# Summing the adaLN products over partitions: VectorE block transposes in place of column-tiled products

## Chip, cores and metric

One core of a Trainium2 chip runs the kernel; the other cores have nothing to do. The metric is the device time of one execution, in microseconds (us). Work is spread over TensorE (PE in the profile; PEld are its weight loads), VectorE (DVE), ScalarE (ACT), GpSimd (POOL), and SyncE (SP), which issues the loads.

## What is computed

Two layers of a conditioned decoder trunk on a sequence of 256 tokens, width 1024, in float32. Each layer has three sublayers: a half-step SwiGLU FFN, a token mixer, another half-step SwiGLU FFN. In front of each stands an RMS norm with a shift and a scale, behind it a gate, and these come from a vector `c`:

```python
mod = (silu(c) @ ada_w[l] + ada_b[l]).reshape(B, 3, 3, 1, D)     # 3 sublayers x (shift, scale, gate)
n = modulate(rmsnorm(h, norm_g[l, 0]), mod[:, 0, 0], mod[:, 0, 1])
h = h + 0.5 * mod[:, 0, 2] * swiglu(n, ffn_w_in[l, 0], ffn_w_out[l, 0])
```

So there are 2 x 3 x 3 = 18 vectors of 1024 values, each a product of a vector of 1024 with a 1024 x 1024 matrix: 4 MB of weights for each and little arithmetic. Two of the 18, shift and scale of the first sublayer, are wanted at once and have a path of their own; the other 16 are the "sets" that this case is about.

## The kernel before

All activations are kept transposed: channels on the 128 partitions in 8 blocks, tokens along the free dimension. Weights come in tiles of 128x1024 float32 through one stream (`Stream`), in one fixed order, 512 KB each. For a product in nearly full precision each tile is split into a high part (`hi`, ScalarE, line 151) and the rest (`lo`, VectorE, line 152), and each block product is three TensorE passes: hi with hi, lo with hi, hi with lo. The stream loads ahead up to RAW_MAX_X = 9 tiles and splits ahead up to SPLIT_AHEAD_X = 7 tiles while the slots of the mixer's tiles are lent to it (`lend`), less otherwise.

The adaLN weights run through the same stream, between the others (`ada_plan` says under which sublayer which set is loaded: five sets under the first FFN, one under the first mixer, four under the second FFN, five under the third, one under the last). An adaLN tile is not split: VectorE multiplies it with `silu(c)` per partition and adds it up in `acc[si, m]`, 128x1024 (lines 274 and 277, 8 tiles to a set). What is left is the sum of `acc` over the 128 partitions. `ada_step` does it two steps of its clock after the last tile of a set, called between blocks of products; `ada_flush` brings the results of a sublayer into the layout that is wanted, channels on partitions, and adds bias and the rest (`md`).

In `ada_step` four products of 128x32 weights, one for each quarter of the columns of `acc`, go to the four column tiles of the array. The weights `hot` are zero but for one column of ones, so set k lands in row k of each tile's 32 output rows; ScalarE or VectorE collects this into `rows`. In `ada_flush` two TensorE transposes turn `rows`, and VectorE picks each set's 8 columns.

The order on TensorE, SyncE and GpSimd is that of the program (`manual_schedule`). VectorE and ScalarE are ordered by a planner at build time, by priority (program order less what `tc.high_priority` gives) among what it takes to be ready; at run time each engine goes through its queue in order. ScalarE is in program order in `start()` too.

In `ffn`, `in_mm(j)` are the 48 products of one block of the input projection (line 660), `evac(j)` the SwiGLU of it (lines 626 to 628 and 597, 598), `out_mm(j)` the 24 products of a block of the output projection (line 606). `ada_step` stands behind `out_mm`, `ada_flush` ahead of the last `out_mm`, which takes two blocks together. `mix` ends in the same way, with step and flush inside its last products. `enter` then needs `md`: it updates h with the gate (line 477), forms `uhi` and `ulo` (lines 479 and 472), and starts the next sublayer's products (line 494). `finish` does the same at the end (line 564).

In `start()`, VectorE forms the first two sets by the own path (lines 398, 400, 776 to 784). There `const_load` loads the constants `cst_t[:, 128:]` (line 407), which hold, among others, four 32x32 identities on top of each other (C_SEL).

Of the kernel before, what the change touches and what calls it, by code (L numbers as in the profile page):

```python
# [18 lines left out]
F32 = mybir.dt.float32  # L19
F32R = mybir.dt.float32r  # L20
AF = mybir.ActivationFunctionType
ALU = mybir.AluOpType
AX = mybir.AxisListType.X
# [12 lines left out]
PRIO_C, PRIO_R, PRIO_T, PRIO_A, PRIO_H, PRIO_M = 300, 200, 400, 50, 50, 300  # L36
# [17 lines left out]
C_VE, C_VM, C_SEL, C_CAUS, C_TRIL, C_BM, C_END = 930, 1058, 1186, 1346, 1474, 1602, 1606  # L54
# [129 lines left out]
def trunk(ctx, tc, xT, pk, cst, ada0, win7, ada, win, wou, mixw, mixv, w1, mp, wsT, lngb, bs, out):  # L184
    nc = tc.nc
    V, A, T, G = nc.vector, nc.scalar, nc.tensor, nc.gpsimd

    cp = ctx.enter_context(tc.tile_pool(name="cp", bufs=1))
# [4 lines left out]
    tp = ctx.enter_context(tc.tile_pool(name="tp", bufs=1))  # L193
# [6 lines left out]
    def uid():  # L200
        cnt["id"] += 1
        return cnt["id"]

    def bank(tag):
        return ps.tile([128, 512], F32, tag=tag, name=f"{tag}_{uid()}")

    def rbank():
        cnt["R"] += 1
        return bank(f"R{cnt['R'] % 4}")

    def s1(dt=F32, tag="s1", bufs=8, n=256):
        return tp.tile([128, n], dt, tag=tag, bufs=bufs, name=f"{tag}_{uid()}")
# [11 lines left out]
    def s2():  # L224
        return s1(F32, "s2", 4, 512)

    def small(n, tag, dt=F32, bufs=2):
        return tp.tile([128, n], dt, tag=tag, bufs=bufs, name=f"{tag}_{uid()}")
# [7 lines left out]
    cst_t = cp.tile([128, C_END], F32, name="cst_t")  # L236
# [4 lines left out]
    ident = cst_t[:, C_ID:C_ID + 128]  # L241
# [3 lines left out]
    nc.sync.dma_start(pk_t, pk)  # L245
    V.memset(ones, 1.0)
    V.memset(mhalf, -0.5)
    hot = cp.tile([128, 64], F32, name="hot")
    V.memset(hot, 0.0)
    V.memset(hot[:, 31:32], 1.0)  # L250
    sel = cp.tile([128, 2], F32, name="sel")
    V.memset(sel, 0.0)
    for t in range(4):
# [3 lines left out]
    def norm_g(si):  # L257
        return pk_t[:, 8 + si * 8:16 + si * 8]
# [3 lines left out]
    def ada_b(si):  # L262
        return pk_t[:, 64 + si * 24:88 + si * 24]


    acc = {}
    mods = {}
    ready, summed, rows, clock = [], [], {}, [0]
# [13 lines left out]
    def ada_step(now=False):  # L282

        clock[0] += 1
        while ready and (now or clock[0] >= ready[0][2]):
            si, m, _ = ready.pop(0)
            k = len(summed)
            p = rbank()
            for t in range(4):
                T.matmul(p[32 * t:32 * t + 32, 0:256], hot[:, 31 - k:63 - k], acc[si, m][:, t * 256:(t + 1) * 256],  # L290
                         start=True, stop=True, tile_position=(0, 32 * t))
            with tc.high_priority(PRIO_M):
                if k == 0:
                    rows["t"] = tp.tile([128, 256], F32, tag="adas", name=f"adas{si}_{m}")
                    A.activation(rows["t"], p[:, 0:256], AF.Copy)
                else:
                    V.tensor_add(rows["t"], rows["t"], p[:, 0:256])
            summed.append((si, m))

    def ada_flush():  # L300

        p = rbank()
        for f in range(2):
            T.transpose(p[:, f * 128:(f + 1) * 128], rows["t"][:, f * 128:(f + 1) * 128], ident)
        with tc.high_priority(PRIO_M):
            for k, (si, m) in enumerate(summed):
                t = cp.tile([128, 8], F32, tag=f"md{si}_{m}", name=f"md{si}_{m}")
                v = p[:, 0:256].rearrange("p (f t r) -> p t f r", f=2, r=32)[:, :, :, k]
                V.tensor_add(t.rearrange("p (t f) -> p t f", f=2), v,
                             ada_b(si)[:, m * 8:(m + 1) * 8].rearrange("p (t f) -> p t f", f=2))  # L310
                if m == 1:
                    V.scalar_tensor_tensor(t, t, 1.0, norm_g(si), op0=ALU.add, op1=ALU.mult)
                elif m == 2:
                    V.tensor_scalar(t, t, 0.5, None, op0=ALU.mult)
                mods[si, m] = t
        summed.clear()
# [88 lines left out]

    def const_load():
        nc.sync.dma_start(cst_t[:, 128:], cst[:, 128:])

    for kb in range(8):
        for k in ((0,), (1, 2), (3,), (4,), (5,), (6,), (7,), ())[kb]:  # L410
            items += [ada0_item(k, 0), ada0_item(k, 1)]
            ada0_last.append(len(items) - 1)
        items += [("w", win7[kb, :, 0:1024], 1024), ("w", win7[kb, :, 1024:], 768)]
        if kb == 3:
            items.append(("call", const_load, ()))
# [199 lines left out]
    def ffn(si, prev):  # L615
# [21 lines left out]
        if si == 0:  # L637
            with tc.manual_schedule(engines=START_ENGINES):
                x, zb = start()
            for j in range(4):  # L640
                evac(j, zb[j])
            accs = [bank(f"A{i}") for i in range(4)]
            for j in range(NS - 1):
                out_mm(j)
                if j + 4 < NS:
                    evac(j + 4, zb[j + 4])
                st.more()
                ada_step()
# [56 lines left out]
        for j in range(NS if si == 0 else 4, NF):  # L705
            r = in_mm(j)
            evac(j, r)
            st.more()
            for k in outs_after(si, j):
                out_mm(k)  # L710
                if k < NF - TAIL:
                    st.more()
                ada_step(k >= NF - TAIL)
        if summed:
            ada_flush()
# [111 lines left out]
    def mix(si, l, prev):  # L827
# [441 lines left out]
        for kb in range(8 - WGROUP):  # L1269
            acc_mm(accs, [(st.next(), mhi[:, kb], mlo[:, kb])], kb == 0, False)  # L1270
            st.more()
            if kb >= 2:
                ada_step()
        Ws = [(st.next(), mhi[:, kb], mlo[:, kb]) for kb in range(8 - WGROUP, 8)]
        acc_mm(accs, Ws, False, True, lambda db: ada_step(True) if db == 0 else ada_flush() if db == 3 and summed else None)
        return accs

# [126 lines left out]
```

## Time and profile before

| | us |
|---|---|
| three runs without profile | 1122.38, 1124.91, 1126.12 (median 1124.91) |
| profiled execution | 1121.94 |
| its span, first to last instruction | 1119.8 |
| TensorE, VectorE, ScalarE busy in the span | 1109.5, 875.0, 601.1 |

A span is one execution as the profiler saw it. TensorE's matmuls are pipelined and overlap in the record, so a duration of one (some 277 ns for 256 columns) is longer than the distance from one to the next. The chain of work is followed back from the last instruction, at each step to what released it or to the instruction before it on its engine; it tells which work the end hangs on.

### The profile page before, as it was taken

How to read it: one execution, taken by the hardware profiler on the slowest of the kernel's cores; microseconds unless marked ns; L12 is line 12 of the kernel's file. 1: busy time of each engine (PE TensorE's matmuls, PEld its weight loads, DVE VectorE, ACT ScalarE, POOL GpSimd, SP SyncE). 2: the span in 40 equal slices, each digit the busy share in tenths (PEclk: the TensorE clock that was granted, in tenths of full speed). 3: DMA queues.
4: the chain of work that ended last, by engine and by line, in shares of the span. 5: the costliest groups of instructions: out<-in, count | busy, mean ns of one | idle time of the engine just before them, and what ended most of it. 6: DMA issues, size and time to landing. Idle time of an engine off the chain costs nothing.

```text
span 1119.8 us, 23472 instructions
## 1 busy us (share of the span) xinstructions
PE 1109.5 (99%) x9542; PEld 1068.0 (95%) x9542; DVE 875.0 (78%) x1495; ACT 601.1 (54%) x1014; POOL 11.2 (1%) x15
## 2 busy tenths in 40 slices
PE   9999999999999999999999999999999999999997
PEld 8999999989999999999999999998899999999997
DVE  6898888998868799787599987868876689755643
ACT  4463435675665655444464443558566657544543
POOL 0000000000000000000000000000000000000000
PEclk9999999999999999999999999999999999999999
DMA  9999889756453669888547977965633373866601
GB/s 370 403 336 353 301 316 362 274 191 228 170 180 123 247 234 407 322 323 314 193 148 293 408 290 286 341 244 188 217 133 132 133 276 139 310 216 243 218 31 38
DMA packets 80379, 278.06 MB, mean 248 GB/s; under 512 B 10768, under 2 KB 11280, under 8 KB 80272
## 3 DMA queue, kind: packets, MB, share of 16 engines
q1 hardware_dynamic: 80272, 276.58, 67.6%
q8 instruction: 74, 1.21, 0.4%
q14 instruction: 33, 0.27, 0.1%
HBM read 275.49 MB, written 1.05 MB: 247 GB/s over the span
## 4 chain that ended last, share of the span: by engine, by line
PE 61%; DVE 1%; DMA 1%; ACT 1%; issue 0%; POOL 0%; DVEq 0%; SPq 0%; ACTq 0%; POOLq 0%
PE R L660 28%; PE A L606 16%; PE A L856 4%; PE R L494 2%; PE A L843 2%; PE A L660 1%; DMA raw<-in_win 1%; PE A L1071 1%; PE R L843 1%; PE R L1071 1%; DVE lo L152 1%; PE R L1208 1%; PE R L1176 1%; PE R L290 1%; PE R L856 1%; PE A L1218 0%
## 5 line engine op out<-in xcount | busy, mean ns | idle before, releaser
L152 DVE TENSOR_TENSOR lo<-raw,hi 128x1024 fp32r<-128x1024 f32 x366 | 443.0, 1215 | 115.9 <-ACT hi L151 72.7
L151 ACT ACTIVATE hi<-raw 128x1024 fp32r<-128x1024 f32 x368 | 381.7, 1048 | 242.3 <-PE R L660 57.6
L606 PE MATMUL A<-s1r,hi 128*128 128x256 f32 x1408 | 252.7, 277 | 0.0
L660 PE MATMUL R<-nhi,hi 128*128 128x256 f32 x1152 | 226.1, 278 | 0.0
L660 PE MATMUL R<-nhi,lo 128*128 128x256 f32 x1152 | 224.9, 276 | 0.0
L660 PE MATMUL R<-nlo,hi 128*128 128x256 f32 x1152 | 224.5, 276 | 0.0
L606 PEld LDWEIGHTS A<-s1r,hi 128*128 128x128 f32 x1408 | 218.0, 188 | 0.6 <-ACT hi L151 0.4
L606 PE MATMUL A<-s1r,lo 128*128 128x256 f32 x704 | 194.9, 277 | 0.0
L660 PEld LDWEIGHTS R<-nhi,hi 128*128 128x128 f32 x1152 | 173.5, 188 | 5.8 <-issue 5.8
L660 PEld LDWEIGHTS R<-nhi,lo 128*128 128x128 f32 x1152 | 173.9, 188 | 0.0
L660 PEld LDWEIGHTS R<-nlo,hi 128*128 128x128 f32 x1152 | 173.6, 188 | 0.0
L277 DVE SCALAR_TENSOR_TENSOR acc<-raw,sc,acc 128x1024 f32<-128x1024 f32 x112 | 143.3, 1279 | 8.6 <-DMA raw<-in_ada 8.2
L606 PEld LDWEIGHTS A<-s1r,lo 128*128 128x128 f32 x704 | 132.2, 188 | 0.0
L626 ACT ACTIVATE s<-R 128x256 f32<-128x256 f32 x75 | 28.3, 378 | 132.8 <-PE R L660 132.8
L856 PE MATMUL A<-nhi,hi 128*128 128x256 f32 x256 | 72.7, 284 | 0.0
L856 PE MATMUL A<-nlo,hi 128*128 128x256 f32 x256 | 70.8, 277 | 0.0
L856 PE MATMUL A<-nhi,lo 128*128 128x256 f32 x256 | 70.8, 277 | 0.0
L628 DVE TENSOR_TENSOR s<-s,R 128x256 f32<-128x256 f32 x75 | 31.2, 416 | 39.1 <-ACT s L626 39.1
L597 ACT ACTIVATE s1r<-s 128x256 fp32r<-128x256 f32 x88 | 36.0, 412 | 35.6 <-DVE s L628 33.9
L856 PEld LDWEIGHTS A<-nhi,hi 128*128 128x128 f32 x256 | 48.1, 188 | 2.1 <-issue 0.3
L856 PEld LDWEIGHTS A<-nhi,lo 128*128 128x128 f32 x256 | 48.2, 188 | 0.0
L856 PEld LDWEIGHTS A<-nlo,hi 128*128 128x128 f32 x256 | 48.1, 188 | 0.0
(274 smaller groups left out, 1598.0 us busy)
## 6 DMA issues: line engine op xcount, KB each, us to landing
raw<-in_win SPq DMA_DIRECT2D x170, 512.0 KB, 5.9
raw<-in_ada SPq DMA_DIRECT2D x144, 512.0 KB, 6.1
raw<-in_mixw SPq DMA_DIRECT2D x92, 512.0 KB, 3.6
raw<-in_wou SPq DMA_DIRECT2D x88, 512.0 KB, 5.9
w<-in_w SPq DMA_DIRECT2D x8, 512.0 KB, 7.4
raw<-in_mixv SPq DMA_DIRECT2D x8, 512.0 KB, 4.9
raw<-in_win SPq DMA_DIRECT2D x8, 384.0 KB, 9.6
h<-in_xT SPq DMA_DIRECT2D x2, 512.0 KB, 4.3
```

Source lines behind the costliest of these rows:

```text
L151: self.nc.scalar.activation(hv, rv, AF.Copy)
L152: self.nc.vector.tensor_sub(lv, rv, hv.bitcast(F32))
L277: V.scalar_tensor_tensor(a, raw[:, :D], sc[:, kb:kb + 1], a, op0=ALU.mult, op1=ALU.add)
L494: T.matmul(ub[u][b][:, 0:SU], w(u, (0, 1, 0)[part], kb, b), (uhi, uhi, ulo)[part][:, kb], start=(kb == 0 and part == 0), stop=(kb == 7 and ...
L597: A.activation(hi_out, src, AF.Copy)
L606: T.matmul(accs[db // 2][:, (db % 2) * S:(db % 2 + 1) * S], w[:, db * 128:(db + 1) * 128], xx, start=(first and i == 0 and p == 0 and db % ...
L626: A.activation(s_, r[:, 0:S], AF.Silu)
L628: V.tensor_mul(g_, s_, r[:, S:2 * S])
L660: T.matmul(r[:, ab * S:(ab + 1) * S], W[:, c0:c0 + 128], xx[:, k], start=(i == 0 and ab == 0), stop=(i == 23), skip_group_check=True)
L843: T.matmul(banks[tt][i][:, 0:cn], xx[:, kb, tt * 128:(tt + 1) * 128], w[:, k, c0:c0 + cn], start=(kb == 0 and p == 0), stop=(kb == 7 and p ...
L856: T.matmul(r[:, b * S:(b + 1) * S], w[:, k], xx[:, k], start=(b == 0 and k == 0 and p == 0), stop=(k == 7 and p == 2), skip_group_check=True)
L1071: T.matmul(r[:, 0:S], w[:, k, b * 128:(b + 1) * 128], xx[:, k], start=(n == 0), stop=(n == 11))
```

## The change

`ada_step` no longer uses TensorE. For each half of `acc`, VectorE transposes it in blocks of 32x32 within 128x512 and adds up each block's rows (32 columns each), which leaves in `rows`, 128 x (set, 32), the sums over each group of 32 partitions. `ada_flush` adds the four groups with one fp32 product for all sets of the sublayer: weights `sel4`, 128x128, which are four identities of 32 beside and on top of each other, and 32 columns for each set. The result has all channels on every group of 32 partitions; four VectorE copies, one a group, pick what belongs there, and the additions of the bias follow. `hot` goes; `sel4` is filled by four VectorE copies out of `cst_t` in `const_load`. The order of the calls and of the loads stays. The first two sets keep their own column-tiled products in `start()`.

```diff
-    hot = cp.tile([128, 64], F32, name="hot")
-    V.memset(hot, 0.0)
-    V.memset(hot[:, 31:32], 1.0)
+    sel4 = cp.tile([128, 128], F32, name="sel4")
...
-            p = rbank()
-            for t in range(4):
-                T.matmul(p[32 * t:32 * t + 32, 0:256], hot[:, 31 - k:63 - k], acc[si, m][:, t * 256:(t + 1) * 256],
-                         start=True, stop=True, tile_position=(0, 32 * t))
-            with tc.high_priority(PRIO_M):
-                if k == 0:
-                    rows["t"] = tp.tile([128, 256], F32, tag="adas", name=f"adas{si}_{m}")
-                    A.activation(rows["t"], p[:, 0:256], AF.Copy)
-                else:
-                    V.tensor_add(rows["t"], rows["t"], p[:, 0:256])
+            a = acc[si, m]
+            if k == 0:
+                rows["t"] = tp.tile([128, 5, 32], F32, tag="adas", name=f"adas{si}_{m}")
+            for c in range(2):
+                t = s2()
+                V.transpose(t, a[:, c * 512:(c + 1) * 512])
+                V.tensor_reduce(rows["t"][:, k, c * 16:(c + 1) * 16], t.rearrange("p (j r) -> p j r", r=32), axis=AX, op=ALU.add)
...
-        for f in range(2):
-            T.transpose(p[:, f * 128:(f + 1) * 128], rows["t"][:, f * 128:(f + 1) * 128], ident)
+        n = len(summed)
+        T.matmul(p[:, 0:n * 32], sel4, rows["t"][:, 0:n].rearrange("p k j -> p (k j)"), start=True, stop=True)
         with tc.high_priority(PRIO_M):
+            v = p[:, 0:n * 32].rearrange("p (k f q) -> p q k f", k=n, q=4)
+            u = small(40, "adac", bufs=1)
+            uv = u[:, 0:n * 8].rearrange("p (k f) -> p k f", f=8)
+            for q in range(4):
+                V.tensor_copy(uv[32 * q:32 * q + 32], v[32 * q:32 * q + 32, q])
...
-                V.tensor_add(t.rearrange("p (t f) -> p t f", f=2), v,
-                             ada_b(si)[:, m * 8:(m + 1) * 8].rearrange("p (t f) -> p t f", f=2))
+                V.tensor_add(t, uv[:, k], ada_b(si)[:, m * 8:(m + 1) * 8])
...
     def const_load():
         nc.sync.dma_start(cst_t[:, 128:], cst[:, 128:])
+        for q in range(4):
+            V.tensor_copy(sel4[:, 32 * q:32 * q + 32], cst_t[:, C_SEL:C_SEL + 32])
```

## Rows read from the trace of the kernel before

**Rows 1.** The page, part 1: busy us, share of the span, instructions.

```profile
PE 1109.5 (99%) x9542; PEld 1068.0 (95%) x9542; DVE 875.0 (78%) x1495; ACT 601.1 (54%) x1014; POOL 11.2 (1%) x15
```

**Rows 2.** The chain of work in order of time: start us, us, what.

```profile
392.47 1.13 DVE lo L152
...
424.22 5.44 PE R L660 x48
...
448.70 0.57 PE R L290 x8
449.27 5.65 PE R L660 x48
...
818.40 1.70 PE R L1104 x16
```

**Rows 3.** Stretches: us, busy us (instructions) of each engine, TensorE clock, DMA share, GB/s.

```profile
20.00:34.00 14.00, 14.00 (x126) 12.50 (x127) 13.93 (x31) 6.46 (x10) 0.00 (x0) 1.00 1.03 407
...
84.00:196.00 112.00, 112.00 (x983) 109.83 (x982) 94.13 (x103) 47.79 (x67) 0.00 (x0) 1.00 0.91 333
616.00:728.00 112.00, 112.00 (x996) 109.31 (x995) 94.41 (x104) 49.98 (x68) 0.00 (x0) 1.00 0.88 331
728.00:749.00 21.00, 21.00 (x188) 21.00 (x187) 10.83 (x16) 9.60 (x14) 0.00 (x0) 1.00 0.66 233
```

**Rows 4.** Timeline of TensorE, three places: start us, us, engine, line, operation, shapes.

```profile
28.82 0.40 PE L792 MATMUL A<-nhi,lo 128*128 128x256 f32 x2
...
203.91 0.27 PE L304 MATMUL R<-cst_t,adas 128*128 128x128 f32 x1
...
449.20 0.50 PE L660 MATMUL R<-nhi,hi 128*128 128x256 f32 x2
449.54 0.39 PE L660 MATMUL R<-nhi,lo 128*128 128x256 f32 x2
```

**Rows 5.** Groups by line and shape: busy us, mean ns, idle before and releaser.

```profile
L290 PE MATMUL R<-acc,hot 128*32 128x256 f32 x128 | 10.2, 391 | 0.0
...
L297 DVE TENSOR_TENSOR adas<-adas,R 128x256 f32<-128x256 f32 x11 | 4.6, 415 | 1.8 <-PE R L290 1.8
...
L995 DVE BATCH_NORM_STATS2 bst<-vz 128x6 f32<-128x512 f32 x4 | 2.6, 686 | 2.2 <-ACT vz L984 2.2
...
L1021 DVE TENSOR_SCALAR vz<-vz,mv,vr 128x512 f32<-128x512 f32 x4 | 2.1, 534 | 0.4 <-POOL vr L1001 0.4
...
L1129 DVE TENSOR_REDUCE sm<-s 128x16 f32<-128x256 f32 x2 | 0.8, 408 | 0.0
...
L1015 DVE COPY kcs<-R 32x64 f32<-32x64 f32 x2 | 0.4, 202 | 0.0
```

**Rows 6.** VectorE's waits, 84 to 196 us, then the whole span: total us, times, longest.

```profile
DVE s L628 <- ACT s L626: 12.8, 12, 2.2
...
DVE s L731 <- DMA h<-in_xT: 3.2, 1, 3.2
```

**Rows 7.** The chain of work in the last 22 us: start us, us, what.

```profile
1103.72 0.22 PE R L304 x2
...
1105.38 0.49 DVE h L564
```

**Rows 8.** Timeline of VectorE, four places; in brackets the idle time before and its releaser.

```profile
25.07 1.22 DVE L152 TENSOR_TENSOR lo<-raw,hi 128x1024 fp32r<-128x1024 f32 x1
...
201.20 0.42 DVE L297 TENSOR_TENSOR adas<-adas,R 128x256 f32<-128x256 f32 x1 [0.39 <-PE R L290]
...
378.43 0.17 DVE L309 TENSOR_TENSOR md<-R,pk_t 128x8 f32<-128x8 f32 x1 [3.70 <-PE R L304]
...
1104.18 0.17 DVE L314 TENSOR_SCALAR md<-md 128x8 f32<-128x8 f32 x1
```

**Rows 9.** The line that loads the constants: SyncE's issue, and issue to landing.

```profile
L407 SPq DMA_DIRECT2D cst_t<-in_cst x1: 328/328/328, 21.3 to 21.3; - x1
...
DMA to landing us min/median/max: 10.1/10.1/10.1
```

More of the change, by code (lines that the diff above doesn't have):

```diff
@@ L302, in ada_flush @@
         p = rbank()
-        for f in range(2):
-            T.transpose(p[:, f * 128:(f + 1) * 128], rows["t"][:, f * 128:(f + 1) * 128], ident)
+        n = len(summed)
+        T.matmul(p[:, 0:n * 32], sel4, rows["t"][:, 0:n].rearrange("p k j -> p (k j)"), start=True, stop=True)
         with tc.high_priority(PRIO_M):
+            v = p[:, 0:n * 32].rearrange("p (k f q) -> p q k f", k=n, q=4)
[3 more added lines that the diff above has]
+                V.tensor_copy(uv[32 * q:32 * q + 32], v[32 * q:32 * q + 32, q])
             for k, (si, m) in enumerate(summed):
                 t = cp.tile([128, 8], F32, tag=f"md{si}_{m}", name=f"md{si}_{m}")
-                v = p[:, 0:256].rearrange("p (f t r) -> p t f r", f=2, r=32)[:, :, :, k]
-                V.tensor_add(t.rearrange("p (t f) -> p t f", f=2), v,
-                             ada_b(si)[:, m * 8:(m + 1) * 8].rearrange("p (t f) -> p t f", f=2))
+                V.tensor_add(t, uv[:, k], ada_b(si)[:, m * 8:(m + 1) * 8])
                 if m == 1:
```

## The prediction

> **What bounds the kernel now.** I read the page first: TensorE is busy for 99% of a span of 1119.8 us, VectorE for 78%, ScalarE for 54% [rows 1]. A busy TensorE may still be one that waits with a matmul open, so I went on to the chain of work in order of time. In the FFN stages it is TensorE from one matmul to the next: 5.44 us for each 48 products of a projection, with nothing between [rows 2]. So a microsecond taken out of TensorE's own queue there is a microsecond of the time, as long as what feeds TensorE keeps up. VectorE feeds it (each weight tile needs a subtraction on line 152), and so does the DMA; that is the question I then put to the table by stretches, where TensorE's granted clock is 1.00 [rows 3].
>
> **What leaves TensorE.** In the same chain each step of the adaLN sums (line 290) stands as 0.57 us, and the 48 products behind it take 5.65 instead of 5.44 us [rows 2]. The timeline shows where: the first two products behind the group take 0.50 us, the next two 0.39 us as usual [rows 4]. A set costs 0.57 + 0.21 = 0.78 us. Line 290 has 128 records [rows 5], 8 in a set [rows 2], so there are 16 sets: 16 x 0.78 = 12.5 us. I count all of it as gained, since TensorE has no gap around these groups.
>
> [...] By the rows, the eight records hold TensorE for 0.57 us and the products behind them for 0.21 us more [rows 2]. [...]
>
> **What comes onto VectorE.** A set gets two block transposes of 128x512 and two sums of 128x512 into 128x16. No row shows a transpose. For the sums there are rows of half the size, 0.408 us for 128x256; statistics over 128x512 took 0.686 us, a scaling of 128x512 0.534 us [rows 5]. From below a transpose costs what the scaling does, 0.53 us; from above I allow it four passes, 4 x 0.68 = 2.7 us. I take 0.68 us, the rows of the same shape that go through it once. The set then costs 4 x 0.68 = 2.7 us; the addition of line 297, 0.414 us in 11 of the 16 sets [rows 5], goes, and five ScalarE copies. Net 2.3 to 2.7 us a set, some 39 us in all, on an engine with 245 us of idle time.
>
> [...]
>
> Does it fit where the sets lie? From 84 to 196 us VectorE was busy for 94.1 of 112 us [rows 3]. Four of the first sublayer's five sets are in there: 4 x 2.4 = 9.6 us, and TensorE's gain makes the stretch 3.1 us shorter: 103.7 of 108.9 us. It fits, with little left, and 12.8 us of the idle time were waits of line 628 for the activation before it, which is to say for TensorE [rows 6]; new work can stand there only if the planner puts it there. From 616 to 728 us, in the third FFN, it was busy for 94.4 us [rows 3], with five sets: 106.4 of 108.1 us. Splits run up to seven tiles ahead (SPLIT_AHEAD_X, line 48), each tile is 24 products, 2.72 us, so a short lag is absorbed, and the third FFN ends in a stretch in which VectorE has 10.2 of 21 us free [rows 3]. I take 0, with bounds of 0 and 7.8 us, which is the gain of the ten sets of the first and third FFN, 10 x 0.78.
>
> **The flush at the end of a sublayer.** Two TensorE transposes, 0.22 us in the chain [rows 7], become one fp32 product of 32 to 160 columns. The nearest row has 16 records of 128x32 in 1.70 us, two records a product, so 0.21 us [rows 2]; I take no difference, five times -0.1 to 0.1. Behind it stand four copies of 32 partitions out of PSUM, ahead of the additions of line 309: 0.202 us for 32x64 is the nearest row [rows 5], in a queue some 0.6 us for four. The scale and shift wait for them, and so h (line 477) and uhi. At the end md is halved by 1104.4 us and h starts at 1105.38 us, when the products of the A bank are done [rows 7, 8]: 1.0 us of cover for 0.6. At the other FFN flushes the 48 products of the last pair go on for 5.4 us behind it. Behind the flush of the first mixer there is little: VectorE works from 378.43 us on [rows 8], and the chain of the later stages begins with its split at 392.47 us [rows 2]. There I count 0.4 us; bounds of 0 and 5 x 0.6 = 3 us.
>
> **The wait in front of the flush.** TensorE works in program order, so the product waits for the last sum, and the products of the last pair of blocks are queued behind it. In three of the five sublayers that have a flush, the last set is summed several blocks of products earlier. In the first FFN the addition that ends the last step is at 201.20 us and the flush at 203.91 us [rows 4, 8], 2.7 us, against 2.3 us of new work if no split stands between: 0.3 us, bounds 0 and 2.5. In the first mixer VectorE is idle for 3.70 us before the flush's addition at 378.43 us [rows 8]: 0.
>
> **The selector.** `hot` and two memsets go; sel4 is filled by four copies of 128x32 out of cst_t. VectorE works in order, so if they stand early in its queue, the splits, the first adaLN terms (lines 398, 400) and the first modulation (lines 776 to 784) are queued behind their wait for that DMA, and TensorE waits for those. The load is issued at 21.3 us and lands 10.1 us later, at 31.4 us [rows 9]; from 20 to 34 us VectorE is busy for 13.93 of 14 us [rows 3]. If the copies stood right behind the issue, near 23 us, VectorE would lose 8 us. TensorE's cover is small: the split that starts at 25.07 us is over at 26.3 us, its first product is at 28.82 us [rows 4, 8], 2.5 us. So the price lies between 0 and about 6 us. Of all VectorE's waits for a DMA the longest is 3.2 us [rows 6]. I take 1 us, 3.2 less most of the cover.
>
> **The sum.** -12.5 + 0 + 0 + 0.4 + 0.3 + 1.0 = -10.8 us. The profiled execution took 1121.94 us (its span and 2.1 us around it), so 1111.1 us; it lies below the lowest of the three runs shown (1122.38). On their median, 1124.91 - 10.8 = 1114.1: forecast **1114 us**.
>
> **Rivals.**
> 1. VectorE becomes the bound in the first and third FFN. For it: 103.7 of 108.9 and 106.4 of 108.1 us by my own price, and idle time that lies in front of line 628. Against it: tiles split ahead, and free stretches behind. The gain of ten sets is lost: -10.8 + 7.8 = -3.0, 1122 us.
> 2. The selector's copies hold VectorE until 31.4 us. For it: an engine busy for 13.93 of 14 us and a load of 10.1 us. Against it: no VectorE instruction of that stretch waits for a DMA before. 6 us instead of 1: 1119 us.
> 3. Slower: a block transpose of four-byte elements takes several passes. The place is the same two stretches. VectorE's idle time there is 17.9 / 5 = 3.6 us a set. A set adds 2 x 1.3 + 2 x 0.68 - 0.4 = 3.6 us with a transpose of 1.3 us; from there on the stretch is longer than before. At 2.7 us it adds 6.4 us, 2.8 too many, 28 us for ten sets; the free stretches take back some, the gain of the other six sets (4.7 us) too: about 1143 us. For it: there is no row. Against it: the rows of 512 elements take 0.53 to 0.69 us [rows 5].
> 4. The column tiles cost only their stream: twice 256 columns, by 5.44 us for 48 products 2 x 0.113 = 0.23 us a set, 3.6 us in all: -3.6 + 1.7 = -1.9, 1123 us. The chain's 0.57 and 0.21 us are against it.
>
> **Chances.** Forecast 0.64, rival 1 0.11, rival 2 0.12, rival 3 0.11, rival 4 0.02. A measurement of this kernel can tell about 0.3%, 3.4 us, from no change, so "faster" is below 1121.5 us: the forecast, 0.10 of rival 2 and 0.04 of rival 1, 0.78. Same: the rest of these and rival 4, 0.11. Slower: rival 3, 0.11. The range goes from 1109 us (the unknown costs at or below zero, and the spread of the runs, 1122.38 to 1126.12) to 1123 us, which takes in rivals 1, 2 and 4; rival 3 and a little of the ends are left out.
>
> **What would show it.** Products at 5.44 us where 0.57 + 5.65 us stood: term one. The mean durations of the transposes and sums: term two. TensorE idle for VectorE between 84 and 196 or 616 and 728 us: rival 1. A VectorE copy that waits for cst_t before 32 us, with TensorE idle behind it: rival 2. A flush product that starts late, behind the last sum: the wait in front of the flush. The prediction is wrong if TensorE's gaps grow by more than 3 us in sum, or if the products stand no closer once the column tiles are gone.

## The result and the profile after

The changed kernel takes 1111.3 us (median of six runs, 1110.96 to 1115.93), the kernel before, beside it on the same chip, 1123.55 us. The ratio is 0.9904, 95% interval 0.9886 to 0.9923: 10.8 us less by the ratio, 12.2 us by the medians. The runs lie on two levels, four of them from 1110.96 to 1111.54 us, two at 1114.71 and 1115.93 us. The profiled one is the slowest, 1115.93 us with a span of 1113.9 us. What the two levels are is part of the answer.

Part 1 of the page after, which answers to [rows 1]: TensorE has 5.4 us less to do, VectorE 34.4 us more.

```profile
PE 1104.1 (99%) x9414; PEld 1070.1 (96%) x9414; DVE 909.4 (82%) x1570; ACT 599.7 (54%) x1009; POOL 11.1 (1%) x15
```

The table by stretches after (columns as in [rows 3]). VectorE went from 94.1 to 102.4 and from 94.4 to 104.8 of 112 us; TensorE stays full.

```profile
84.00:196.00 112.00, 111.81 (x952) 111.61 (x950) 102.44 (x119) 46.25 (x65) 0.00 (x0) 1.00 0.91 330
616.00:728.00 112.00, 112.00 (x990) 112.00 (x990) 104.84 (x121) 51.80 (x70) 0.00 (x0) 1.00 0.91 332
```

The chain after at the place of [rows 2] (start us, us, what). Where 0.57 us of line 290 and 5.65 us behind it stood, two projections stand at 5.44 us with an output block between.

```profile
440.48 5.44 PE R L660 x48
445.92 2.72 PE A L606 x24
448.64 5.44 PE R L660 x48
```

The new lines after (count, min/median/max ns, first and last start us): the transposes, the sums, the product of the flush, its copies, and the copies that fill `sel4`, which the profile calls `sel`.

```profile
L291 DVE STREAM_TRANSPOSE s<-acc x32: 665/703/714, 92.3 to 1038.8; 128x512 f32<-128x512 f32 x32
...
L292 DVE TENSOR_REDUCE adas<-s x32: 643/679/689, 96.6 to 1039.9; 128x16 f32<-128x512 f32 x32
...
L299 PE MATMUL R<-adas,sel x10: 193/276/300, 203.7 to 1097.4; 128*128 128x160 f32 x4, 128*128 128x32 f32 x4, 128*128 128x128 f32 x2
...
L305 DVE COPY adac<-R x20: 153/180/207, 205.1 to 1098.2; 32x40 f32<-32x40 f32 x8, 32x8 f32<-32x8 f32 x8, 32x32 f32<-32x32 f32 x4
...
L407 DVE COPY sel<-cst_t x4: 173/174/175, 33.7 to 34.0; 128x32 f32<-128x32 f32 x4
```

TensorE's waits after, over the whole span (total us, times, longest). One wait is for the split of line 152, 0.2 us; none is at the flush.

```profile
PE R L579 <- DVE s L569: 1.8, 1, 1.8
...
PE A L453 <- DVE s L452: 0.7, 3, 0.3
PE A L660 <- ACT nhi L526: 0.6, 1, 0.6
...
PE R L660 <- DVE lo L152: 0.2, 1, 0.2
```

The time of each sublayer, from TensorE's first product of it in the timeline to the first of the next (the first FFN from its first output product, about 62 us; the last up to line 579; us), shows where the profiled executions differ. The other kernels are those of the experiments below.

| | FFN 1 | mixer 1 | FFN 2 | FFN 3 | mixer 2 | FFN 4 |
|---|---|---|---|---|---|---|
| sets summed | 5 | 1 | 4 | 5 | 0 | 1 |
| before | 148.1 | 174.1 | 185.35 | 185.27 | 172.3 | 185.40 |
| after | 147.3 | 174.0 | 182.41 | 181.71 | 173.6 | 184.53 |
| no_sums | 142.1 | 174.25 | 182.47 | 181.78 | 173.6 | 184.51 |
| sums_twice | 150.45 | | 182.43 | 184.70 | | |
| pe_kept | 148.15 | 175.3 | 185.55 | 185.63 | 173.6 | 185.40 |
| before_again | 145.9 | 174.1 | 188.3 | 185.26 | 172.3 | 185.43 |
| same_addr | 143.3 | 173.3 | 182.25 | 181.92 | 173.25 | 184.51 |
| one_break | 143.2 | 174.1 | 182.44 | 181.71 | 173.6 | 184.50 |

In FFN 2, 3 and 4 the gain is there: 2.94, 3.56 and 0.87 us for 4, 5 and 1 sets. In FFN 1, with five sets, only 0.8 us can be seen, and the second mixer, which sums none, lost 1.3 us. So the questions were: is it VectorE's new work that eats the gain of FFN 1 (rival 1), and is the gain elsewhere what it was taken for?

### The profile page after: what moved, and what is told of

Its sections match the earlier page's. It is cut to its first block, busy times and chain, and to the rows that moved or that the text cites. A ratio compares the mean times of both kernels' runs of the same rounds, so it can differ in the third digit from the quotient of the medians.

```text
span 1113.9 us, 23286 instructions
## 1 busy us (share of the span) xinstructions
PE 1104.1 (99%) x9414; PEld 1070.1 (96%) x9414; DVE 909.4 (82%) x1570; ACT 599.7 (54%) x1009; POOL 11.1 (1%) x15
## 4 chain that ended last, share of the span: by engine, by line
PE 92%; DVE 2%; DMA 2%; ACT 1%; issue 1%; POOL 1%; SPq 0%; POOLq 0%; DVEq 0%; ACTq 0%
PE R L660 35%; PE A L606 23%; PE A L856 8%; PE A L843 4%; PE A L1071 2%; PE A L792 2%; PE R L843 2%; PE R L494 2%; PE R L1071 2%; PE R L792 1%; PE A L660 1%; DMA raw<-in_win 1%; DMA ln<-in_lngb 1%; PE R L1208 1%; PE R L1176 1%; PE R L856 1%
## 5 line engine op out<-in xcount | busy, mean ns | idle before, releaser
L660 PEld LDWEIGHTS R<-nhi,lo 128*128 128x128 f32 x1152 | 174.1, 188 | 0.4 <-DVE lo L152 0.4
L660 PEld LDWEIGHTS R<-nhi,hi 128*128 128x128 f32 x1152 | 174.0, 188 | 0.0
L275 DVE SCALAR_TENSOR_TENSOR acc<-raw,sc,acc 128x1024 f32<-128x1024 f32 x112 | 143.3, 1280 | 7.8 <-DMA raw<-in_ada 7.6
```

The source lines that it names most:

```text
L275: V.scalar_tensor_tensor(a, raw[:, :D], sc[:, kb:kb + 1], a, op0=ALU.mult, op1=ALU.add)
L660: T.matmul(r[:, ab * S:(ab + 1) * S], W[:, c0:c0 + 128], xx[:, k], start=(i == 0 and ab == 0), stop=(i == 23), skip_group_check=True)
```

## The experiments

**The sums left out (no_sums).** The transposes and sums give way to a memset of the same row, so the 16 sets are missing from what is computed; flush, copies and sel4 stay.

```diff
-            for c in range(2):
-                t = s2()
-                V.transpose(t, a[:, c * 512:(c + 1) * 512])
-                V.tensor_reduce(rows["t"][:, k, c * 16:(c + 1) * 16], t.rearrange("p (j r) -> p j r", r=32), axis=AX, op=ALU.add)
+            V.memset(rows["t"][:, k], 0.0)
```

> The changed kernel without the transposes and sums: the rows that go into the flush product are set to zero, so the 16 adaLN sets are left out of the result. Theory: VectorE's new work (16 x 4 x 0.69 = 44 us) is hidden, and the time is that of the changed kernel, 1111 us, within 1.5 us. Rival 1 of the prediction in a weak form: VectorE's load still costs part of the gain in the first and third FFN; then 1105 to 1108 us.

Measured: 1115.75 us (1110.66 to 1117.77), ratio 0.994, 0.9916 to 0.9964; the profiled run 1110.66 us. With the transposes and sums gone VectorE is busy for 875.7 instead of 909.4 us, but the kernel is no faster; its median is even 4 us above that of the changed kernel beside it (after_again, below), and none of its slower runs has a profile. By stages, FFN 2, 3 and 4 agree with after to 0.1 us. There the sums are hidden. Only FFN 1 differs, 142.1 against 147.3 us, and no wait accounts for 5.2 us. The chains of both in that stage show what does:

```profile
96.50 5.65 PE R L660 x48
104.98 5.65 PE R L660 x48
```

is after, and no_sums (its line 657) has

```profile
95.06 5.44 PE R L657 x48
103.22 5.44 PE R L657 x48
```

The same products run at two paces: 8.48 us for a projection and an output block, 72 products, in after, 8.16 us in no_sums, 0.118 and 0.113 us a product. The granted clock is 1.00 in both.

The pace makes 4.8 of the 5.2 us (below). The rest is the wait of after for line 152. It doesn't stand in no_sums, whose 144 products of the projections from 176.66 us on run through in 16.37 us, and it is longer where the pace is the fast one, as in one_break (the changed kernel with one small addition, below). TensorE there, with the two transposes on VectorE that stand ahead of the split:

```profile
184.57 0.39 PE L665 MATMUL R<-nhi,hi 128*128 128x256 f32 x2
185.38 0.50 PE L665 MATMUL R<-nhi,lo 128*128 128x256 f32 x2 [0.42 <-DVE lo L152]
...
182.92 1.30 DVE L291 STREAM_TRANSPOSE s<-acc 128x512 f32<-128x512 f32 x2
184.15 1.19 DVE L152 TENSOR_TENSOR lo<-raw,hi 128x1024 fp32r<-128x1024 f32 x1
```

The second pair starts 0.81 us after the first instead of 2 x 0.113, and takes 0.50 instead of 0.39 us: 0.7 us lost. In after, at the slow pace, it is 0.5 us. So the sums are not free in FFN 1.

**The changed kernel again (after_again).** No edit.

> The changed kernel once more, for a second profile. In the first profile (1115.93 us) the distance from one 256-column product to the next is 0.118 us from 54 to 190 us and 0.113 us behind a gap of 0.47 us at 189.8 us; in the kernel before the same change comes at 122 us, behind a group of line 290. Theory: this slow pace ends by chance behind an interruption of TensorE, and makes the spread of the runs (1111 to 1116 us): a run near 1111 us has some 800 to 1000 products less at 0.118 us, 3.6 to 4.5 us. Rival: the spread comes from elsewhere (the start, the loads): then the profile of a run near 1111 us has the slow pace up to 190 us as well.

Measured: 1111.52 us; 1110.79, 1111.00, 1111.52, 1111.52, and 1116.10, 1116.11, against 1122.2 us before; ratio 0.992, 0.9895 to 0.9944. The same two levels. The profiled run is one of the two at 1116 us, and its chain too has 5.65 us for 48 products from one end of FFN 1 to the other. 0.32 us for every 72 products, some 15 times from 62 to 190 us, are 4.8 us: the distance between the levels.

**The sums twice (sums_twice).**

```diff
-            for c in range(2):
+            for c in (0, 1, 0, 1):
```

> The changed kernel with each transpose and sum done twice. Theory of a limit close by: from 84 to 196 us VectorE then wants 102.4 + 4 x 2.8 = 113.6 of 112 us, from 616 to 728 us 104.8 + 5 x 2.8 = 118.8 of 112 us, so TensorE waits there for VectorE and the time rises by 4 to 9 us, to 1115 to 1120 us. Rival: tiles split ahead and free stretches take it all: 1111 to 1113 us.

Measured: 1122.7 us (ten runs, 1119.96 to 1125.62), ratio 1.0004, 0.9985 to 1.0023: 11 us over after, more than expected. Its stretches:

```profile
84.00:196.00 112.00, 106.85 (x916) 105.54 (x915) 110.31 (x133) 45.65 (x63) 0.00 (x0) 0.98 0.92 330
616.00:728.00 112.00, 110.59 (x964) 109.50 (x964) 110.93 (x134) 47.72 (x65) 0.00 (x0) 1.00 0.89 328
```

and TensorE's waits over its whole span:

```profile
PE A L606 <- ACT s1r L597: 3.1, 4, 1.7
...
PE R L660 <- DVE lo L152: 1.8, 2, 1.4
PE A L606 <- DVE s1r L598: 1.5, 1, 1.5
```

VectorE is now at 110.3 and 110.9 of 112 us and TensorE has holes for it. FFN 1 is 7 us longer than in the executions that also ran it at 0.113 us a product (150.45 against 143.2 and 143.3), FFN 3 3.0 us; FFN 2, with four sets, nothing. Some 1.2 us of the 7, an estimate, are the clock: behind waits of up to 1.7 us TensorE's granted clock was 0.53 from 180 to 181 us and 0.69 from 181 to 185 us, and 11 products there stand 0.213 us apart instead of 0.113. Over the stretch from 84 to 196 us the clock is 0.98, in after 1.00. What lowered it no run here shows. So rival 1 is real, but at the price of this change it shows only as the one wait of 0.5 to 0.7 us: with one dose the two stretches have 9.6 and 7.2 us left.

**The column-tiled products put back beside VectorE's sums (pe_kept).** Their results are not used.

```diff
+            p = rbank()
+            for t in range(4):
+                T.matmul(p[32 * t:32 * t + 32, 0:256], hot[:, 31 - k:63 - k], a[:, t * 256:(t + 1) * 256],
+                         start=True, stop=True, tile_position=(0, 32 * t))
```

> The changed kernel with the old column-tiled products of line 290 put back beside VectorE's sums; nobody reads them. Theory: all of the gain is TensorE's time, 16 x 0.78 = 12.5 us, so this kernel stands at 1111 + 12 = 1122 to 1124 us, as the kernel before, though VectorE does all its new work; in the profile the products behind each group take 5.65 us for 48 again. And the interruptions come back: a slow pace (0.118 us a product) that enters the first FFN ends at one of the groups at 104, 122 or 147 us. Rival: part of the gain comes from the rest of the change (waits of VectorE and ScalarE for TensorE that are gone): then 1116 to 1120 us.

Measured: 1125.41 us (1122.5 to 1126.75), ratio 1.0022, 1.0009 to 1.0035: a little above the 1122 to 1124 us expected, and 2.5 us (1.0 to 3.9) above before. Taken from the two ratios, 13.2 us more than after. By stages against after: 3.14, 3.92 and 0.87 us for 4, 5 and 1 sets in FFN 2, 3 and 4, 0.78 to 0.87 us a set. Its chain, the place of [rows 2] again:

```profile
450.05 0.57 PE R L292 x8
450.62 5.65 PE R L667 x48
```

(This 5.65 us is 5.44 us and the 0.21 us behind the group, not the slow pace.) So all that the change gained is these products' time on TensorE, and the rest of the change costs some 2.5 us. And here as in before, the slow pace of FFN 1 ended at the second of these groups. TensorE's timeline of before:

```profile
121.41 0.40 PE L606 MATMUL A<-s1r,hi 128*128 128x256 f32 x2
...
121.98 0.64 PE L290 MATMUL R<-acc,hot 128*32 128x256 f32 x8
122.55 0.51 PE L660 MATMUL R<-nhi,hi 128*128 128x256 f32 x2
122.89 0.39 PE L660 MATMUL R<-nhi,lo 128*128 128x256 f32 x2
```

Ahead of the group two products stand as 0.40 us, behind it as 0.39 us. The group at 104.25 us had not ended it.

**The kernel before again (before_again).** No edit, a single run.

> The kernel before once more, for a second profile. If the slow pace in the first FFN is chance, it starts near 53 us and ends at another one of the groups of line 290 than that at 122 us, or does not come at all (the runs of before lie between 1119.7 and 1127.8 us); if it is a matter of the code it ends at 122 us again. The blocks of line 856 in the mixers: 5.64 us each if the alternation of the changed kernel is its own, some of 5.85 us if that is chance too.

Measured: 1122.67 us. FFN 1 ran at the faster pace, and FFN 2 at the slower one until a line-290 group at 474.7 us, past the one at 448.5 us: 3 us more in that stage (table). So before has both paces too, in other places from run to run; its projection in that stretch took 5.65 us, with no edit.

**Breaks put in (pe_breaks, pe_breaks_2, one_break).** If an interruption can end the slow pace, TensorE was only given too few of them. Small groups of column-tiled products stand behind the first blocks of the first FFN (this code runs in that FFN alone, so one_break costs one break, not the four its expectation counts).

```diff
                 ada_step()
+                if j < 4:
+                    b_ = bank("R3")
+                    for t in range(4):
+                        T.matmul(b_[32 * t:32 * t + 32, 0:32], ones[:, 0:32], ones[:, 0:32], start=True, stop=True,
+                                 tile_position=(0, 32 * t))
```

one_break has `if j == 0:` there.

> The changed kernel with four small interruptions of TensorE early in the first FFN (behind each of the first four blocks of line 606, 62 to 75 us): four column-tiled products of 32 columns each, whose result nobody reads. Theory: each costs 0.4 to 0.7 us, and one of them ends the slow pace of 0.118 us a product near 70 us instead of by chance at 120 or 190 us: up to 1000 products x 4.5 ns = 4.5 us back; the runs lie together at 1110 to 1113 us, with none at 1115. Rival: the pace has nothing to do with interruptions: 2 to 3 us above the changed kernel, 1113 to 1118 us, and the pace in the profile changes elsewhere.

> The kernel with four breaks an FFN again. Theory (an interruption can end the slow pace): no run more than 2.5 us above the fastest, as before (1111.99 to 1114.69), and if the profile has a slow stretch of the first FFN it ends at one of the four groups. Rival: with six more runs, two or three lie 4 to 5 us above the others, and the first set of runs had none by chance.

> The changed kernel with one group of four column-tiled products of 32 columns behind the first out_mm block of each FFN. It costs about 0.5 us an FFN, 2 us in all. Theory: the slow pace that enters the first FFN (0.118 us a product, up to 5 us over the stage) is ended, or not, at an interruption of TensorE. With one early interruption more the runs lie between those of the changed kernel (5 of 12 runs near 1115 to 1116, the others near 1111) and those with four breaks: at most 1 or 2 of 6 above 1114.5, the rest near 1112 to 1113. Rival: the two levels belong to the execution as a whole and have nothing to do with interruptions: again a third to a half of the runs 4 to 5 us above the others, near 1117.

Measured: 1112.3 us (1111.99 to 1114.69; ratio 0.9919, 0.9898 to 0.9939), again 1113.72 us (1111.52 to 1114.22; 0.9906, 0.9886 to 0.9927), and with one break 1111.18 us (1110.65 to 1111.46; 0.9887, 0.9868 to 0.9906). No run of the three is at 1115 us or above, though in each set with four breaks one lies 2.7 us above the lowest. But in all three profiles the pace was already the fast one from about 62 us on, ahead of the first break, so none of them shows a break ending the slow one.

**Where the tiles lie (layout, same_addr, before_pad).** The mixers have both paces as well, in a fixed pattern. In the chain of the second mixer after, the groups of 48 products of line 856 alternate; in before each took 5.64 to 5.66 us.

```profile
839.66 5.85 PE A L856 x48
...
847.90 5.64 PE A L856 x48
...
855.93 5.85 PE A L856 x48
```

The change also moves tiles: sel4 is 256 bytes larger than hot, the collected sums are smaller, `adac` is new. layout gives hot its place back and puts sel4 among the working tiles:

```diff
-    sel4 = cp.tile([128, 128], F32, name="sel4")
+    hot = cp.tile([128, 64], F32, name="hot")
+    V.memset(hot, 0.0)
+    V.memset(hot[:, 31:32], 1.0)
+    sel4 = tp.tile([128, 128], F32, name="sel4")
```

> The changed kernel with the places in SBUF as before up to the last pool: hot stays (128x64, set and not read), sel4 is in the last pool. In the profiles of the changed kernel every other block of line 856 in the attention loops of both mixers takes 5.85 instead of 5.64 us for 48 products, in the one of before all take 5.64. Theory: that comes from the shift of the operands' addresses by 256 bytes; then this kernel has 5.64 throughout, and its mixers take 0.8 to 1.3 us less each, 1109 to 1110 us for the quick runs. Rival: it is the phase in which TensorE comes out of an interruption; then the blocks alternate here as well, and the time is that of the changed kernel.

Measured: 1115.92 us (1111.42 to 1116.5), ratio 0.9934, 0.9915 to 0.9953, and the same alternation. But tp's tiles still lay elsewhere than in before. same_addr mends that: sel4 and `adac` go to a pool behind all others, the collected sums take their old size.

```diff
+    zp = ctx.enter_context(tc.tile_pool(name="zp", bufs=1))
...
-    sel4 = cp.tile([128, 128], F32, name="sel4")
+    hot = cp.tile([128, 64], F32, name="hot")
+    V.memset(hot, 0.0)
+    V.memset(hot[:, 31:32], 1.0)
+    sel4 = zp.tile([128, 128], F32, name="sel4")
...
-                rows["t"] = tp.tile([128, 5, 32], F32, tag="adas", name=f"adas{si}_{m}")
+                rows["t"] = tp.tile([128, 8, 32], F32, tag="adas", name=f"adas{si}_{m}")
...
-            u = small(40, "adac", bufs=1)
+            u = zp.tile([128, 40], F32, tag="adac", name="adac")
```

> The changed kernel with its tiles put back to where they lay before: hot is allocated again (and unused but for its memsets), the collected sums take the old size, and sel4 and the small tile of the flush lie in a pool of their own behind all others. Nothing that runs is otherwise changed. Two paces of TensorE (0.113 and 0.118 us from one 256-column product to the next) are in the traces; in the mixers the changed kernel has 5.85 us for every other group of 48 products of line 856, the kernel before 5.64 us for each. Theory A: the pace hangs on where the tiles lie. Then all groups of the mixers take 5.64 us here, about 1.3 us less in the second mixer and 0.8 in the first, and the median is about 1110. Rival B: it hangs on what runs in front of it (the new flush, the order on the engines). Then every other group takes 5.85 us as in the changed kernel, median 1111 to 1112, with single runs at 1116.

before_pad shifts the later pools of the kernel before by 256 bytes:

```diff
-    xp_.tile([128, 48], F32, tag="pad", name="pad_x")
+    xp_.tile([128, 112], F32, tag="pad", name="pad_x")
```

> The kernel before with 64 more columns of unused space in its pad tile, so that the tiles of the later pools lie 256 bytes further, as the change moves them by making sel4 256 bytes larger than hot. Nothing that runs is changed. Theory A (the pace of TensorE hangs on where the tiles lie): the mixers' groups of 48 products of line 856 alternate between 5.64 and 5.85 us, and the time is 1 to 2 us above the kernel before, ratio 1.001. Rival B: as the kernel before, 5.64 us for each group, ratio 1.000 within its interval.

Measured: same_addr 1113.99 us (1109.83 to 1116.28; ratio 0.9907, 0.9885 to 0.993), before_pad 1123.82 us (1119.84 to 1125.65; 0.9998, 0.9985 to 1.001). In the chain of same_addr (its line 860) every group of the mixer is back at 5.64 us:

```profile
834.25 5.64 PE A L860 x48
842.27 5.64 PE A L860 x48
```

before_pad has 5.64 us throughout too. So the mixers' pattern goes with where the tiles lie, not with the new flush or the order of work, which same_addr shares with after; but not with any shift: 256 bytes for the later pools alone did nothing. Which tile counts was not told apart. For the time it is about 1 us: by the table 0.7 us in the first mixer and 0.35 us in the second, and the lowest run of same_addr is 1109.83 us, against 1110.79 to 1110.96 in after. The two levels are still there in same_addr, so its median missed the 1110 us of theory A.

**Both at once (addr_break).** same_addr with one break in the first FFN.

> Both at once: the changed kernel with its tiles where they lay before the change (as in same_addr), and one group of four column-tiled products of 32 columns behind the first out_mm block of the first FFN (it stands in the first FFN alone, and costs about 0.5 us there). Theory: the places of the tiles take 5.64 us for each group of the mixers, some 2 us less than the changed kernel, and the early break leaves no run with the slow pace through the first FFN: the median is about 1109.5 and no run lies above 1112. Rival (the tight runs with one break were chance, the places of the tiles do nothing): two or more of the runs lie at 1113 to 1116, as in same_addr, and the median is 1111 to 1114.

Measured: 1109.59 us, the lowest median of all; 1109.07 to 1109.72 in four runs, but 1112.77 and 1116.15 in two; ratio 0.9909, 0.9885 to 0.9933. The mixers' part of the theory held. The break's part fell: one early break doesn't keep a run from the upper level. With breaks 1 of 20 runs was at 1115 us or above, without them 9 of 24 (after, after_again, layout and same_addr); no_sums, without a break too, has 4 of 6. That an interruption of one's own can end the slow pace would fit these counts, and is not shown (the sets ran on different chips). In the profiled run of addr_break the pace went from fast to slow at 176.5 us, long after the break, with no wait there: two products 0.120 and 0.121 us apart, and 0.118 us from then on. By intervals addr_break is not told from after.

## Why the prediction was right, and where its steps were off

The forecast was 1114 us, 10.8 us below before; it came to 1111.3 us, 10.8 us by the ratio. The mechanism was right: TensorE's time for the column tiles came back, and TensorE's waits grew only from 4.2 to 4.7 us over the span. Not every term was right on the way.

**What leaves TensorE** was right: 0.78 us a set. pe_kept gives it back at 0.78 to 0.87 us a set, 16 sets were 12.5 us in the sum, and the two ratios give 13.2 us for them. Rival 4, four tiles at the price of their stream, falls with the 0.57 and 5.65 us that stand there again. The tiles do run side by side: in before four records of the group at 448.63 us, 0.39 us each, lie within 0.42 us, and all eight within 0.64 us.

**What comes onto VectorE** was right: 0.703 us for a transpose and 0.679 us for a sum, forecast 0.68 us each. For the transpose that figure was an estimate from the rows of the same shape, and it took what the statistics over 128x512 take, 0.686 us [rows 5]. Rival 3 needed 1.3 us. (Its 17.9 us of idle time for five sets are those of the first FFN's stretch, which holds four; the third FFN's 17.6 us for five give nearly the same limit.) It fits where it lies, as priced at zero, in FFN 2 to 4, which don't change when it is left out (no_sums). In FFN 1 the zero was wrong by 0.5 to 0.7 us: rival 1 in a weak form. That is the one wait of after, which the chain has at 187 to 190 us:

```profile
181.31 5.67 PE R L660 x48
...
187.75 0.95 DVE s L291 x2
...
188.97 1.20 DVE lo L152
...
190.21 8.22 PE R L660 x70
```

Two transposes stand in VectorE's queue ahead of a split, and TensorE sits idle for it. The wait is in all the profiles of the changed kernel and of its variants with breaks or moved tiles; pe_kept, whose TensorE is slower, doesn't have it. The pace behind it was the fast one in after, the slow one in after_again and same_addr. sums_twice shows rival 1 in full at twice this work.

**The flush** was mis-sized in its copies. The product itself took the place of the transposes at next to no cost (0.27 for 0.22 us). I put the copies at 0.4 us, behind the first mixer, and at nothing at the other FFNs, because 5.4 us of products go on behind them. That was the step that was furthest off: those products cover the copies themselves, but what follows them, h, uhi, the squares and the statistics up to line 452, is a chain of its own that goes on under the next sublayer's first products, and TensorE comes to line 453 before it is done. VectorE's timeline after the first FFN's flush (203.71 us; 203.91 us before), in after:

```profile
205.11 0.82 DVE L305 COPY adac<-R 32x40 f32<-32x40 f32 x4
...
206.62 0.48 DVE L477 SCALAR_TENSOR_TENSOR h<-A,md,h 128x256 f32<-128x256 f32 x1
...
218.65 0.48 DVE L452 TENSOR_SCALAR s<-cst_t,rstd 128x128 f32<-128x128 f32 x2 [0.59 <-POOL rstd L440]
```

and in before:

```profile
205.93 0.48 DVE L477 SCALAR_TENSOR_TENSOR h<-A,md,h 128x256 f32<-128x256 f32 x1
...
218.14 0.48 DVE L452 TENSOR_SCALAR s<-cst_t,rstd 128x128 f32<-128x128 f32 x2 [0.59 <-POOL rstd L440]
```

The copies take 0.82 us; counted from the flush, h starts 0.9 us and line 452 0.7 us later. At the entries of the third FFN and the second mixer line 452 comes 0.7 us later too. At the third FFN, in after, the chain itself goes through the copies:

```profile
561.59 0.18 DVE adac L305
...
562.80 0.50 DVE h L477
...
573.30 1.55 POOL rstd L440
...
574.87 0.30 DVE s L452
```

At the second mixer the chain has, from the last pair's products to the second half of line 494, 15.03 us in before and 15.49 us in after:

```profile
749.02 5.48 PE A L606 x48
...
763.61 0.45 PE A L453 x4
764.05 2.88 PE R L494 x24
```

before, and after

```profile
742.30 5.47 PE A L606 x48
...
756.74 0.30 DVE s L452
...
757.08 0.71 PE A L453 x4
757.79 2.88 PE R L494 x24
```

(In between, that chain names a load of `ln`, which landed 0.12 us after VectorE's last step ahead of `rstd`; in no_sums and pe_kept, with the same 14.8 us from the last pair to line 453, it names VectorE.) That is some 0.5 us at each of two mixers, by the distance of the same products, and 0.3 us at the third FFN. At the place where I had put 0.4 us, behind the first mixer, TensorE's gap in front of line 660 grew from 0.69 to 0.87 us, start to start. In all some 1.5 us for 0.4, inside the bounds of 0 and 3. No run leaves out the copies alone; the order of VectorE's queue behind them changed a little too.

**The wait in front of the flush** was nothing, forecast 0.3: no wait of line 299 is among TensorE's. VectorE's timeline has no transpose and no sum between 194 us and the flush.

**The selector** was mis-sized on the safe side. The four copies stand at 33.71 us, in one row without idle time ahead of it, after the 31.4 us at which the load of [rows 9] had landed. VectorE never waits for cst_t, and rival 2 falls. The first product of line 606 came at 62.2 us (61.5 us before), 61.3 us in same_addr, 61.4 us in pe_kept: between -0.2 and 0.7 us, forecast 1.0. before_pad, which runs the same work as before, had 62.7 us, so this is within what the start varies by itself.

**Not in the sum** was the pace. In its profiled FFN 1 before ran at the slower pace up to 122 us, after up to 190 us: by 0.32 us for 72 products, 8.48 us, that is 2.3 and 4.8 us of those stages. The prediction read 5.44 us for 48 products in the FFN stages; up to 122 us the trace of before has 5.65. That is why FFN 1 seems to have gained only 0.8 us: with both at the faster pace it is 145.9 us (before_again) against 143.2 us (one_break, 0.4 us of it the break), 3.1 us of the 3.9 expected. The wait for the split is the rest; no_sums, also at the faster pace and without the wait, is at 142.1 us, 3.8 us below. The line-290 groups that the change removed were also the places at which a slow stretch ended, in the profiles of before, pe_kept and before_again. The mixers' tiles cost another 1 us. Against the sum the copies cost 1.1 us more, the wait for the split 0.5 to 0.7 us, the mixers' tiles 1 us; the selector and the wait in front of the flush cost some 1 us less. The parts then add up to a gain of some 9 us, an estimate from these figures; measured are 10.8 us, with an interval of 8.7 to 12.8. That the forecast met 10.8 exactly is luck: the pace alone moves a run by up to 5 us. The 2.5 us by which pe_kept lies above before fit the copies and the tiles, 1.5 and 1 us. Of the second mixer's 1.3 us, 0.5 us are the copies and 0.4 us the two groups at 5.85 us; 0.4 us stay open.

## What to carry to other kernels

Read what a small group in another tile shape costs a full TensorE from the chain, its own time and what it adds to the products behind it (here 0.57 and 0.21 us), and move it to an engine with room if the stretch where it lies, not the span, has that room. Even there, look at what stands ahead of the next instruction that the full engine needs: two transposes in front of one split made a wait of 0.5 to 0.7 us in a stretch with 9.6 us free. When work is added ahead of a transition, follow the dependent chain up to the point where the busiest engine next asks for its result; products that run beside the first step of that chain don't cover the last. Before a difference of a few microseconds is explained by the edit, see whether the same products run at the same pace in both traces, and whether the edit moved tiles.

## What the runs showed of the hardware

TensorE has two paces for the same stream of 128x128 weights and 256 columns at a granted clock of 1.00: 5.44 and 5.65 us for 48 products, 0.113 and 0.118 us a product. In the long streams a pace mostly lasts until TensorE is interrupted, and may or may not change there: it passed the group at 104.25 us and changed at the one at 121.98 us in before; at the wait for line 152 it went from slow to fast in after, from fast to slow in same_addr, and stayed slow in after_again. Once, in addr_break at 176.5 us, it changed without a wait. In the first FFN this made 5 us from one run to the next of the same kernel; in the mixers it went with where the tiles lie (5.64 and 5.85 us, the same in nine profiles of kernels with moved tiles, absent in five with the old places or the later pools shifted alone). What sets it inside the engine no run here shows.

Four 32-row column tiles that follow a stream of full-array products cost 0.57 us and 0.21 us more in the products behind, in before and put back in pe_kept alike. With 32 columns instead of 256 the group still costs 0.4 us (the first 144 products of line 606 take 17.04 us in one_break, 16.64 us in before_again), so by this estimate about half of the price does not go with the columns that are streamed.
